# Gathering a unit's rows earlier on the GpSimd queue of a fused decoder block

## The chip, the core and the metric

The kernel runs on one core of a Trainium2 chip. The metric is device time in microseconds (us). Before the change it is 1564.48 us, the median of 3 runs (1563.86 to 1565.02). The profile is one execution, taken by the hardware profiler. Its engines are PE (TensorE: matrix products and transposes; PEld is its weight load), DVE (VectorE), ACT (ScalarE), POOL (GpSimd) and SP (SyncE, which here only issues DMAs). Each engine works through its own list of instructions in order; semaphores join the lists.

## The reference

One decoder layer over 512 tokens of width 1024: a mixer (sparse attention beside a pooling branch), then a mixture of experts, each followed by a LayerNorm. The change touches the experts alone:

```python
logits = (hf @ w_router).astype(jnp.float32) + b_router.astype(jnp.float32)
top_logit, top_e = lax.top_k(logits, TOP_K_EXPERTS)          # 4 of 32
gate = jax.nn.softmax(top_logit, axis=-1)
...
gu = xb @ w_gate_up[e] + b_gate_up[e]                         # xb: the expert's tokens
x_glu, x_lin = jnp.split(gu, 2, axis=-1)
x_glu = jnp.minimum(x_glu, SWIGLU_LIMIT)
x_lin = jnp.clip(x_lin, -SWIGLU_LIMIT, SWIGLU_LIMIT)
act = x_glu * jax.nn.sigmoid(SWIGLU_ALPHA * x_glu) * (x_lin + 1.0)
return act @ w_down[e] + b_down[e]
```

Each token's four results are weighted by `gate` and summed. Everything is float32; one expert's weights are 12 MB.

## The kernel before

The mixer fills the first 450 us or so; the rest are 32 *jobs*, one for each expert, ranked by how many tokens chose it. `KINDS` (line 63) gives every job a shape. A narrow job (N) has at most 64 tokens: its products use the weights as they were loaded, line 1404. A wide job (W) has at most 128: each weight chunk is first split into a high and a low part, by ACT (line 225) and DVE (line 234), and PE makes three products, line 1394. A triple job (T, jobs 8 and 19) is two *units* in one, a wide and a narrow one. All other jobs are one unit. The kinds in order are NNNNNNNN T NN WWWWW NNN T NN WWWW N WWW NN.

**Phases.** A job j has an up phase ("G", j), eight weight chunks of 1 MB, and a down phase ("D", j), four. `phases_of` interleaves them: ..., G j, D j-1, G j+1, D j, ...; around a triple job two of one kind follow each other (D 7, G 8, G 9, D 8, G 10, D 9, G 11, D 10, ...). A phase begins on PE with a product for the bias, line 1421. The weights are loaded by SP into a ring of tiles (`raw`), always a certain number of chunks ahead: a chunk's load is issued when an older chunk has been used up.

**A unit's rows.** A unit's tokens are found by a list of row numbers (`sl_wr`) and gate weights (`sl_gt`), which DVE writes for four units at a time (`unit_batch`, lines 1261 to 1278). `gather` (line 1373) is an indirect DMA that POOL issues: it fetches the listed rows from DRAM (`h2_rows`, shown as h_rows) into the tile `xg`. There is room for one unit there, or two of a triple job, so a gather waits on POOL until PE has transposed the rows that lay there before. `turn_steps` are those transposes (line 1331, from xg to a PSUM bank `ps_c`), four for a narrow unit and eight for a wide one, and the copies to `xT` or `xTn` (lines 1345, 1347, 1348). They are hooked into the down phase that stands before the unit's own up phase: job j's rows are turned in D j-2.

**What POOL does besides.** In the up phase's wake two swiglu products (lines 1464, 1465) of each half, and for each down phase `finish_down`: ACT copies the result out of PSUM, scaled (line 1489), POOL multiplies it by gate2 (line 1491 for a wide result in tile `y`, line 1495 in two halves for a narrow one in `yn` or `y`), and an indirect DMA adds it to the rows of `acc_rows` in DRAM (line 1470, the scatter).

**What sets the order.** `hook(ph, k, f)` runs f behind chunk k of phase ph, and the order in which the hooks run is the order of instructions on every engine. The swiglu of an up phase and `finish_down` of a down phase come behind all hooks of their phase. Before the change a unit's gather is hooked to chunk 0 of the phase before the one in which its rows are turned (`late_hook`), behind all other hooks of that chunk.

Of the kernel before, what the change touches and what calls it, by code (L numbers as in the profile page):

```python
# [36 lines left out]
E = 32  # L37
# [33 lines left out]
def tile_hybrid_block(ctx, tc, x, c, w_ada, b_ada, w_in, kv_norm_g, w_uk, w_uv, w_pool_group,  # L71
# [24 lines left out]
    def slot(shape, tag, dt=F32, bufs=1, name=None):  # L96
        pool = stream if tag in LASTING else ft_last if tag in LAST else ft
        return pool.tile(shape, dt, name=name or tag, tag=tag, bufs=bufs)
# [68 lines left out]
    def phases_of():  # L167


        order, late = [], None  # L170
        for j in range(E):
            if j in TRIPLE + (FIRST, E - 1):
                order += [late, ("G", j)]
            else:
                order += [("G", j)] + ([late] if late else [])
            late = ("D", j)
        return order + [late]
# [334 lines left out]
    units = [("ki", split_ki, whole, HD + H, True)]  # L512
# [225 lines left out]
    up, us = slot([P, PAD + S], "u"), slot([P, 2, PAD + S], "usum")  # L738
# [54 lines left out]
    for g in range(4):  # L793
# [12 lines left out]
        for i in range(2):  # L806
            n = 2 * g + i
            v = yb[n // 4][:, n % 4, :]
# [227 lines left out]
    phases = phases_of()  # L1036
# [210 lines left out]
    def mt(shape, tag, dt=F32, bufs=1, name=None):  # L1247
        return (mp if tag in AT_ONCE else mp_rest).tile(shape, dt, name=name or tag, tag=tag, bufs=bufs)
# [32 lines left out]
    def units_of(j):  # L1281
        return [(j, b) for b in range(1 + (j in TRIPLE))]

    def is_narrow(unit):
        return unit[0] in NARROW or unit[1] > 0

    units = [u for j in range(E) for u in units_of(j)]
# [25 lines left out]
    def unit_batch(us):  # L1313
        def col(i):
            j, b = units[us[i]]
            place = pos1[:, :, BASE + j] if j < FIRST else moe["place"][:, :, j]
            if b == 0:
                return place
            second = mt([P, NT], "second")
            nc.vector.tensor_scalar(second, place, float(P), None, op0=OP.subtract)  # L1320
            return second
        return batch(us, col, lambda i, t: aux[:, t, units[us[i]][0], :], 
                     narrow=[is_narrow(units[u]) for u in us])
# [37 lines left out]
    def shared_tile():  # L1361

        if not shared:
            shared.append(stream.tile([P, 2048], F32, name="xg", tag=ROWS[0], bufs=1))
            nc.gpsimd.memset(shared[0][:, 0:1536], 0.0)
        return shared[0]

    def gather(key, narrow, second=False):

        at = 1024 if second else 0  # L1370
        assert all(at != v[0] for v in held.values())
        v = shared_tile()[:, at:at + (512 if narrow else 1024)]
        nc.gpsimd.indirect_dma_start(out=v, out_offset=None, in_=in_halves if narrow else h2_rows[:, :],
                                     in_offset=bass.IndirectOffsetOnAxis(ap=lists[key][0], axis=0),
                                     bounds_check=(2 * S if narrow else S) - 1, oob_is_err=False)
        held[key] = at, v
# [274 lines left out]
    v = mt([P, 1, 3], "sl_v0")  # L1651
# [29 lines left out]
    def hook(ph, k, f):  # L1681
        hooks[ph].setdefault(k, []).append(f)

    gathers = []

    def late_hook(*args):
        gathers.append(args)

    first_unit = {j: units.index((j, 0)) for j in range(E)}
    xTs, acts, aTs = {(0, 0): xT}, {}, {}  # L1690

    def turn_steps(unit):

        fs, narrow = [], is_narrow(unit)

        def begin():
            xTs[unit], steps = gathered(units.index(unit), narrow, unit[1] > 0 or unit[0] in (1, FIRST + 1))
            fs.extend(steps)
            fs.pop(0)()
        return [begin] + [lambda: fs.pop(0)() for _ in range(1 if narrow else 3)]  # L1700

    def act_steps(unit):

        fs, narrow = [], is_narrow(unit)

        def begin():
            aTs[unit] = act_pair(unit[1] > 0 or unit[0] + 1 in TRIPLE + (FIRST, E - 1), narrow)
            for i in range(1 if narrow else 2):
                fs.extend(half_T(acts[unit][i], aTs[unit], i))
            fs.pop(0)()  # L1710
        return [begin] + [lambda: fs.pop(0)() for _ in range(1 if narrow else 3)]

    def spread(ph, ks, steps):
        for i, f in enumerate(steps):
            hook(ph, ks[i * len(ks) // len(steps)], f)

    for i, (kind, j) in enumerate(phases):
        before = phases[i - 1]
        if kind == "G" and j:
            at, ks = before, (0, 1, 1, 2) if before[0] == "D" else (4, 5, 5, 6)  # L1720
            if j in TRIPLE:
                at, ks = ("G", j - 1), (3, 4, 4, 5, 6, 7)
            elif j - 1 in TRIPLE:
                at, ks = ("D", j - 2), (0, 1)
            spread(at, ks, [f for u in units_of(j) for f in turn_steps(u)])
            if j > 1:
                for u in units_of(j):
                    late_hook(phases[phases.index(at) - 1], 0, lambda u=u: gather(units.index(u), is_narrow(u), u[1] > 0))
        elif kind == "D" and j < E - 1:
            spread(before, (3, 4, 5, 6, 6, 7) if j in TRIPLE else (1, 2, 2, 3) if before[0] == "G" else (3,), [f for u in units_of(j) for f in act_steps(u)])  # L1730
    first, second = unit_batch([1]), unit_batch([2])
# [3 lines left out]
    u = 3  # L1735
    while u < len(units):
        j = units[u][0]
        us = list(range(u, min(u + NB, len(units))))
        fs = unit_batch(us)
        for k, f in zip((0, 1, 2, 3), fs[:-2]):  # L1740
            hook(("G", j - 2), k, f)
        hook(("G", j - 2), 4, fs[-2])
        hook(phases[phases.index(("G", j - 2)) + 1], 0, fs[-1])
        u = us[-1] + 1
    for args in gathers:
        hook(*args)
    for j in range(1, E):
        if KINDS[j] != "W":
            hook(("G", j - 1), 2, lambda j=j: pick_halves(j))
# [24 lines left out]
    for ph in phases:  # L1774
        kind, j = ph
        last, us = j == E - 1, units_of(j)
# [132 lines left out]
```

## Time and profile before

| | |
|---|---|
| median of 3 runs | 1564.48 us |
| the profiled execution | 1565.03 us, span 1563.2 us |
| PE busy | 1451.2 us, 93% of the span |
| DVE, ACT, POOL busy | 58%, 40%, 30% |
| granted TensorE clock, mean | 0.970 of full speed |
| DMA | 489.96 MB, mean 313 GB/s |
| gathers of line 1373 | 33 |

The profile shows spans of instructions, and before each the idle time of its engine and what ended it. Issuing a DMA counts as busy on POOL; the transfer itself runs on the core's 16 DMA engines, and its landing is what others wait for. The DMA share in the windows view is the mean busy share of these engines; it can pass 1 a little.

### The profile page before, as it was taken

The numbers are of one execution on the slowest core, as the hardware profiler recorded it, in microseconds if no ns is written. First come the engines' busy times: TensorE is split into PE (matmuls) and PEld (weight loads), VectorE is DVE, ScalarE is ACT, GpSimd is POOL, SyncE is SP. The second block draws the span as 40 slices with busy tenths as digits, with TensorE's granted clock in tenths as the row PEclk, the third lists the DMA queues.
The fourth block names the chain that finished last, engine by engine and source line by source line (L and its number), as shares of the span: only waits on it lengthen the run. The fifth ranks groups of instructions, "written<-read, shape, count | busy, mean of one in ns | idle before, by whom it ended". The sixth has DMA issues, their size and how long they took to land. (4 is left out here: it accounts for less than half of the span.)

```text
span 1563.2 us, 18968 instructions
## 1 busy us (share of the span) xinstructions
PE 1451.2 (93%) x6821; PEld 884.6 (57%) x6821; DVE 913.4 (58%) x1262; ACT 626.5 (40%) x725; POOL 467.0 (30%) x338
## 2 busy tenths in 40 slices
PE   7999999998979998789889999999988999999995
PEld 6766766667843332244356777434435677567551
DVE  6558877567843111054159999404415899589613
ACT  2344234462111101143147776314314677567521
POOL 2200000023522232223324444332232444444332
PEclk8999999999969999999999999999998999999998
DMA  9874521044679999999999899999989989999993
GB/s 290 265 253 135 190 91 55 29 135 189 229 253 416 406 403 410 409 408 362 328 400 404 328 369 363 365 398 406 400 321 386 404 310 365 363 403 395 370 393 137
DMA packets 123377, 489.96 MB, mean 313 GB/s; under 512 B 12513, under 2 KB 42861, under 8 KB 88464
## 3 DMA queue, kind: packets, MB, share of 16 engines
q1 hardware_dynamic: 110832, 445.25, 72.8%
q0 software_dynamic: 12304, 43.27, 9.5%
q8 instruction: 55, 0.90, 0.2%
q14 instruction: 42, 0.34, 0.1%
q10 hardware_dynamic: 144, 0.20, 0.0%
HBM read 473.36 MB, written 19.20 MB: 315 GB/s over the span
## 5 line engine op out<-in xcount | busy, mean ns | idle before, releaser
L234 DVE TENSOR_TENSOR w_lo<-raw,w_hi 128x2048 fp32r<-128x2048 f32 x168 | 419.4, 2520 | 93.9 <-ACT w_hi L225 93.8
L225 ACT ACTIVATE w_hi<-raw 128x2048 fp32r<-128x2048 f32 x168 | 320.2, 1914 | 110.2 <-PE ps_a L1394 91.5
L1404 PE MATMUL ps_a<-raw,xTn 128*64 128x512 f32 x1024 | 237.4, 606 | 11.4 <-DMA raw<-in_w_gate_up_dram 11.4
L1394 PE MATMUL ps_a<-w_hi,xT 128*128 128x512 f32 x896 | 234.0, 404 | 3.5 <-ACT w_hi L225 3.5
L1464 POOL TENSOR_TENSOR sw_l<-sw_l,sw_g 128x512 f32<-128x512 f32 x47 | 88.3, 1879 | 447.6 <-DVE sw_l L1461 393.9
L1394 PEld LDWEIGHTS ps_a<-w_hi,xT 128*128 128x128 f32 x896 | 166.4, 190 | 54.0 <-ACT w_hi L225 11.4
L563 PE MATMUL ps_a<-h_part,wp 128*128 128x512 f32 (+1 forms) x672 | 167.3, 404 | 3.6 <-POOL h_part L500 2.1
L1459 DVE TENSOR_SCALAR sw_g<-ps_a 128x512 f32<-128x512 f32 x46 | 31.6, 687 | 235.1 <-PE ps_a L1404 199.6
L1404 PEld LDWEIGHTS ps_a<-raw,xTn 128*64 128x64 f32 x1024 | 68.8, 138 | 145.2 <-issue 119.8
L563 PEld LDWEIGHTS ps_a<-h_part,wp 128*128 128x128 f32 (+1 forms) x672 | 125.5, 189 | 45.0 <-issue 11.3
L1404 PE MATMUL ps_b<-raw,aT 128*64 128x512 f32 x576 | 137.3, 610 | 11.8 <-DMA raw<-in_w_down_dram 10.0
L1394 PE MATMUL ps_a<-w_lo,xT 128*128 128x512 f32 x448 | 124.3, 400 | 1.8 <-DVE w_lo L234 1.8
L1394 PE MATMUL ps_b<-w_hi,aT 128*128 128x512 f32 x448 | 125.8, 403 | 0.0
L1394 PEld LDWEIGHTS ps_a<-w_lo,xT 128*128 128x128 f32 x448 | 84.8, 190 | 24.3 <-DVE w_lo L234 4.3
L1460 ACT ACTIVATE sw_l<-ps_a,ones 128x512 f32<-128x512 f32 x46 | 31.4, 682 | 161.9 <-PE ps_a L1404 109.9
L1394 PEld LDWEIGHTS ps_b<-w_hi,aT 128*128 128x128 f32 x448 | 81.5, 188 | 23.0 <-issue 6.2
L1404 PEld LDWEIGHTS ps_b<-raw,aT 128*64 128x64 f32 x576 | 37.6, 138 | 87.1 <-issue 59.8
L1495 POOL TENSOR_TENSOR yn<-yn,gate 64x512 f32<-64x512 f32 x30 | 49.5, 1650 | 111.2 <-ACT yn L1489 87.8
L1465 POOL TENSOR_TENSOR sw_l<-sw_l,xg 128x512 f32<-128x512 f32 x47 | 75.1, 1597 | 3.7
L1394 PE MATMUL ps_b<-w_lo,aT 128*128 128x512 f32 x224 | 70.8, 398 | 1.5 <-DVE w_lo L234 1.5
L1348 DVE TENSOR_TENSOR xT<-ps_c,xT 128x512 fp32r<-128x512 f32 x28 | 19.1, 683 | 72.1 <-ACT xT L1347 72.1
L1491 POOL TENSOR_TENSOR y<-y,gate 128x1024 f32<-128x1024 f32 x14 | 37.7, 2693 | 75.7 <-ACT y L1489 75.7
(400 smaller groups left out, 1914.2 us busy)
## 6 DMA issues: line engine op xcount, KB each, us to landing
raw<-in_w_gate_up_dram SPq DMA_DIRECT2D x256, 1024.0 KB, 11.7
raw<-in_w_down_dram SPq DMA_DIRECT2D x128, 1024.0 KB, 9.2
ada<-in_w_ada_dram POOLq DMA_DIRECT2D x16, 1024.0 KB, 5.3
raw<-in_w_in_dram SPq DMA_DIRECT2D x14, 1024.0 KB, 9.0
raw<-in_w_ada_dram SPq DMA_DIRECT2D x32, 256.0 KB, 5.4
raw<-in_w_out_dram SPq DMA_DIRECT2D x4, 1024.0 KB, 5.4
x<-in_x_dram SPq DMA_DIRECT2D x8, 256.0 KB, 7.8
raw<-in_w_branch_pool_dram SPq DMA_DIRECT2D x2, 1024.0 KB, 5.3
```

The lines of the kernel that those rows point to most:

```text
L225: nc.scalar.activation(c["hi"], c["w"], AF.Copy)
L234: nc.vector.tensor_sub(c["lo"], c["w"], c["hi"].bitcast(F32))
L563: nc.tensor.matmul(ps, w[:, part, k, :], h(k), start=(k == part == 0 and h is hh), stop=(k == last and h is hl))
L1348: nc.vector.tensor_sub(pair[:, 1, ks, :], ps[0], pair[:, 0, ks, :].bitcast(F32))
L1394: nc.tensor.matmul(ps[i], a[:, part, k + j, :], m[:, cs], start=first and j == 0 and part == 1, stop=last and j == 4 // n - 1 and m is lo)
L1404: nc.tensor.matmul(ps[i][h * 64:(h + 1) * 64], a[:, kk, c * 64:(c + 1) * 64], w["w"][:, cs], start=first and j == 0, stop=last and j == 4 ...
L1459: nc.vector.tensor_scalar(g, ps[i], LIMIT, None, op0=OP.min)
L1460: nc.scalar.activation(l, ps[len(ps) // 2 + i], AF.Identity, bias=ones[:, 0:1])
L1464: eng.tensor_mul(l, l, g)
L1465: eng.tensor_mul(l, l, sig)
L1491: nc.gpsimd.tensor_mul(y, y, gate2)
L1495: nc.gpsimd.tensor_mul(y[rows], y[rows], gate2[rows, h * 512:(h + 1) * 512])
```

## The change

A unit's gather is now hooked to the place at which the rows of the preceding job have been turned (`turned[j - 1]`: the phase and the last chunk of those steps), or to the place at which its own list is made (`listed`), whichever is later. The hooks are still added last.

```diff
-    gathers = []
-
-    def late_hook(*args):
-        gathers.append(args)
-
     first_unit = {j: units.index((j, 0)) for j in range(E)}
+    listed = {2: (phases.index(("G", 1)), 2)}
...
+    turned = {}
     for i, (kind, j) in enumerate(phases):
...
             spread(at, ks, [f for u in units_of(j) for f in turn_steps(u)])
-            if j > 1:
-                for u in units_of(j):
-                    late_hook(phases[phases.index(at) - 1], 0, lambda u=u: gather(units.index(u), is_narrow(u), u[1] > 0))
+            turned[j] = phases.index(at), ks[-1]
...
-        hook(phases[phases.index(("G", j - 2)) + 1], 0, fs[-1])
+        after = phases.index(("G", j - 2)) + 1
+        hook(phases[after], 0, fs[-1])
+        listed.update({v: (after, 0) for v in us})
         u = us[-1] + 1
-    for args in gathers:
-        hook(*args)
+
+    for j in range(2, E):
+        for u in units_of(j):
+            p, k = max(turned[j - 1], listed.get(units.index(u), (0, 0)))
+            hook(phases[p], k, lambda u=u: gather(units.index(u), is_narrow(u), u[1] > 0))
```

On PE, DVE, ACT and SP the same instructions stand in the same order as before. On POOL they differ in where the gathers (line 1373) stand. The first place is POOL around jobs 8 to 11, from the swiglu of triple job 8 on; the two gathers are those of job 10 (128x512) and of job 11, the first wide one (128x1024). Before:

```order
L1465 TENSOR_TENSOR sw_l<-sw_l,xg 128x512
L1373 DMA xg<-h_rows,sl_wr 128x512
L1464 TENSOR_TENSOR sw_l<-sw_l,sw_g 128x512
L1465 TENSOR_TENSOR sw_l<-sw_l,xg 128x512
L1491 TENSOR_TENSOR y<-y,gate_3549 128x1024
L1470 DMA acc_rows<-y,sl_wr 640x1024
L1495 TENSOR_TENSOR yn<-yn,gate_3549 64x512 x2
L1470 DMA acc_rows<-yn,sl_wr 1280x512
L1373 DMA xg<-h_rows,sl_wr 128x1024
L1464 TENSOR_TENSOR sw_l<-sw_l,sw_g 128x512
```

The same place of POOL's list after the change:

```order
L1465 TENSOR_TENSOR sw_l<-sw_l,xg 128x512
L1373 DMA xg<-h_rows,sl_wr 128x512
L1464 TENSOR_TENSOR sw_l<-sw_l,sw_g 128x512
L1465 TENSOR_TENSOR sw_l<-sw_l,xg 128x512
L1373 DMA xg<-h_rows,sl_wr 128x1024
L1491 TENSOR_TENSOR y<-y,gate_3549 128x1024
L1470 DMA acc_rows<-y,sl_wr 640x1024
L1495 TENSOR_TENSOR yn<-yn,gate_3549 64x512 x2
L1470 DMA acc_rows<-yn,sl_wr 1280x512
L1464 TENSOR_TENSOR sw_l<-sw_l,sw_g 128x512
```

The gather of job 11 has moved ahead of both results of job 8 and their scatters; job 10's has not moved. The same ten rows stand around jobs 19 to 22.

The second place is POOL in the early run of narrow jobs, the gathers of jobs 6 and 7 and of the two units of triple job 8. Before:

```order
L1495 TENSOR_TENSOR yn<-yn,gate_3549 64x512 x2
L1470 DMA acc_rows<-yn,sl_wr 1280x512
L1373 DMA xg<-h_rows,sl_wr 128x512
L1464 TENSOR_TENSOR sw_l<-sw_l,sw_g 128x512
L1465 TENSOR_TENSOR sw_l<-sw_l,xg 128x512
L1495 TENSOR_TENSOR yn<-yn,gate_3549 64x512 x2
L1470 DMA acc_rows<-yn,sl_wr 1280x512
L1373 DMA xg<-h_rows,sl_wr 128x512
L1464 TENSOR_TENSOR sw_l<-sw_l,sw_g 128x512
L1465 TENSOR_TENSOR sw_l<-sw_l,xg 128x512
L1373 DMA xg<-h_rows,sl_wr 128x1024
L1373 DMA xg<-h_rows,sl_wr 128x512
```

And after:

```order
L1373 DMA xg<-h_rows,sl_wr 128x512
L1495 TENSOR_TENSOR yn<-yn,gate_3549 64x512 x2
L1470 DMA acc_rows<-yn,sl_wr 1280x512
L1464 TENSOR_TENSOR sw_l<-sw_l,sw_g 128x512
L1465 TENSOR_TENSOR sw_l<-sw_l,xg 128x512
L1373 DMA xg<-h_rows,sl_wr 128x512
L1495 TENSOR_TENSOR yn<-yn,gate_3549 64x512 x2
L1470 DMA acc_rows<-yn,sl_wr 1280x512
L1464 TENSOR_TENSOR sw_l<-sw_l,sw_g 128x512
L1465 TENSOR_TENSOR sw_l<-sw_l,xg 128x512
L1373 DMA xg<-h_rows,sl_wr 128x1024
L1373 DMA xg<-h_rows,sl_wr 128x512
```

Here a gather has changed places with the multiply and the scatter in front of it; those of the triple job stay.

## Rows read from the trace of the kernel before

**Rows 1.** Waits of PE, whole run: engine, line, for whom: us in total, times, longest.
```profile
PE ps_c L1331 <- DMA xg<-h_rows,sl_wr: 20.3, 3, 10.0
```
**Rows 2.** PE's timeline, jobs 8 to 11: start us, us, instruction [idle before, ended by].
```profile
743.33 0.66 PE L1331 MATMUL ps_c<-ident,xg 128*128 128x128 f32 x4
...
773.58 0.50 PE L1421 MATMUL ps_b<-bias,pick_n 128*128 128x512 f32 x1
...
785.62 1.08 PE L1331 MATMUL ps_c<-ident,xg 128*128 128x128 f32 x4 [9.67 <-DMA xg<-h_rows,sl_wr]
...
793.66 0.73 PE L1421 MATMUL ps_a<-bias,p_pick 64*128 64x512 f32 x4
```
**Rows 3.** PE's timeline, jobs 20 to 22.
```profile
1164.75 0.50 PE L1421 MATMUL ps_b<-bias,pick_n 128*128 128x512 f32 x1
...
1177.12 1.09 PE L1331 MATMUL ps_c<-ident,xg 128*128 128x128 f32 x4 [10.00 <-DMA xg<-h_rows,sl_wr]
...
1185.67 0.73 PE L1421 MATMUL ps_a<-bias,p_pick 64*128 64x512 f32 x4
```
**Rows 4.** PE's timeline, job 10's down phase and the start of the next.
```profile
817.19 0.40 PE L1421 MATMUL ps_b<-bias,pick_n 128*128 128x512 f32 x1
...
826.01 0.73 PE L1421 MATMUL ps_a<-bias,p_pick 64*128 64x512 f32 x4
```
**Rows 5.** POOL's timeline, jobs 8 to 11.
```profile
728.58 1.07 POOL L1373 DMA_INDIRECT xg<-h_rows,sl_wr  x1 [0.15 <-DVE sl_gt L1277]
...
742.91 1.27 POOL L1465 TENSOR_TENSOR sw_l<-sw_l,xg 128x512 f32<-128x512 f32 x1
...
760.30 1.60 POOL L1470 DMA_INDIRECT acc_rows<-y,sl_wr  x1 [0.28 <-POOL y L1491]
...
770.43 1.27 POOL L1495 TENSOR_TENSOR yn<-yn,gate 64x512 f32<-64x512 f32 x1 [7.23 <-DMA acc_rows<-y,sl_wr]
...
773.88 1.09 POOL L1373 DMA_INDIRECT xg<-h_rows,sl_wr  x1 [0.30 <-PE ps_a L1404]
```
**Rows 6.** POOL's timeline, jobs 20 to 22.
```profile
1134.09 1.26 POOL L1465 TENSOR_TENSOR sw_l<-sw_l,xg 128x512 f32<-128x512 f32 x1
...
1165.96 1.06 POOL L1373 DMA_INDIRECT xg<-h_rows,sl_wr  x1 [0.30 <-issue]
```
**Rows 7.** Line 1373: duration ns min/median/max; who waited for it, us, times; landing.
```profile
L1373 POOL DMA_INDIRECT xg<-h_rows,sl_wr x33: 1010/1077/2956, 455.3 to 1491.2; - x33
...
  POOL yn L1495: 7.2, 3
  POOL y L1495: 6.3, 1
...
DMA to landing us min/median/max: 2.9/10.0/13.1
```
**Rows 8.** Windows: stretch, us, busy us of engines, PEclk (granted clock), DMA share, GB/s.
```profile
776.00:786.00 10.00, 0.38 (x2) 0.41 (x3) 0.00 (x0) 0.00 (x0) 1.56 (x2) 0.62 1.03 394
786.00:986.00 200.00, 196.64 (x891) 143.04 (x891) 175.14 (x134) 134.21 (x109) 85.50 (x40) 0.99 0.96 367
986.00:1066.00 80.00, 76.98 (x363) 30.97 (x359) 18.37 (x27) 18.55 (x23) 26.02 (x18) 1.00 1.02 397
...
1178.00:1478.00 300.00, 296.59 (x1343) 209.97 (x1344) 248.45 (x183) 194.18 (x158) 125.11 (x59) 0.99 0.97 375
```
**Rows 9.** SP's issues of job 11's up weights, and the page's landing of such loads.
```profile
762.66 13.67 SPq L139 DMA_DIRECT2D raw<-in_w_gate_up_dram  x8
...
raw<-in_w_gate_up_dram SPq DMA_DIRECT2D x256, 1024.0 KB, 11.7
```
**Rows 10.** POOL's timeline in the early narrow run.
```profile
564.19 1.27 POOL L1465 TENSOR_TENSOR sw_l<-sw_l,xg 128x512 f32<-128x512 f32 x1
...
573.57 1.59 POOL L1470 DMA_INDIRECT acc_rows<-yn,sl_wr  x1 [0.28 <-POOL yn L1495]
...
599.76 2.60 POOL L1495 TENSOR_TENSOR yn<-yn,gate 64x512 f32<-64x512 f32 x2 [7.27 <-ACT yn L1489]
```

## The prediction

> **What bounds the kernel now.** I read the list of what TensorE (PE) waited for first. Its longest entry is a pair of waits of some 10 us each, by the row transposes of line 1331 for the landing of a gather (xg<-h_rows): 20.3 us over three times [rows 1]. Then the PE timeline around them. The first stands in job 9's down phase, 775.95 to 785.62, before the transposes of job 11's rows; the second in job 20's, 1167.12 to 1177.12, before job 22's [rows 2, 3]. Both are the first wide job after the two triple jobs (8 and 19). What has to be seen there is that the transposes stand after the first of the phase's four weight chunks, so the three others wait behind them on PE although they need nothing of the gather.
>
> The POOL timeline says why the gather is late [rows 5]. It stands behind job 8's two results (the multiplies by gate2 and the scatters); the second half of the second multiply waited 7.23 us until the first scatter had landed (770.43), and the gather left at 773.88. Its list was made long before: the gather of job 10, whose list belongs to the same batch of four, left at 728.58 as soon as that batch's last row was written. Job 10's rows were turned at 743.33 to 743.99 [rows 2].
>
> Last the windows of the weight stream [rows 8]. From 786 to 986, the first run of wide jobs, the DMA engines are busy 0.96 of the time and from 1178 to 1478 0.97, while a run of narrow jobs (986 to 1066) shows 1.02, the full stream. So PE sets the pace after either wait, and the stream has some time to spare, though little.
>
> **The change, part by part.** PE, VectorE, ScalarE and the SP queue hold the same instructions in the same order in both kernels. On POOL no instruction is added or taken out; 25 of the main loop's 33 gathers move forward: 18 past one multiply and its scatter, 4 past a swiglu pair, the last past a multiply, its scatter and a swiglu pair, and those of jobs 11 and 22 past two multiplies and two scatters.
>
> *Jobs 11 and 22.* In its new place the gather of job 11 waits for three things: its list (done by 728.58), the landing of the gather before (728.58 plus 13.1 at the longest, 741.7) and the transposes of job 10's rows (743.99). POOL itself is free at 742.91 + 1.27 = 744.18 [rows 5]. So it leaves near 744.2 instead of 773.88, and lands at 757.3 with the longest landing seen [rows 7], 18.6 us before PE asks at 775.95. For job 22 POOL is free at 1134.09 + 1.26 = 1135.35 [rows 6]; 13.1 later is 1148.5, also 18.6 us before 1167.12. Neither wait remains in part.
>
> What they cost now is read from the whole phase, since PE came back slow. Job 9's down phase lasts from bias to bias 793.66 - 773.58 = 20.08 us and job 20's 1185.67 - 1164.75 = 20.92 [rows 2, 3]. Job 10's, with the same narrow products and the same turning of wide rows but no wait, lasts 826.01 - 817.19 = 8.82 [rows 4]. The differences are 11.26 and 12.10, together 23.4 us. The bare waits are 9.67 + 10.00 = 19.7; the other 3.7 is the clock. PE did no matmul from 776 to 785, the granted clock of that stretch is 0.62, between the levels 2.4 and 1.2 GHz [rows 8], and after it four transposes took 1.08 us, where the four at 743.33 took 0.66 [rows 2]. That part cannot be less than nothing; it is 3.7 if PE is never idle there and keeps its clock, which I take.
>
> *Is what follows ready 11 us earlier?* Job 11's eight weight chunks are issued from 762.66 on; with the median landing of 11.7 the first is there at 774.4 [rows 9], when the split into hi and lo could start at about 777. They are just in time, with a later chunk perhaps waiting a microsecond, so between 0 and some 5 us of the gain may be lost at once. I take 0.4, and 23.0 for both places.
>
> *Does the stream follow?* PE's lead eats into loaded chunks, and the stream must win it back before the next narrow run, where PE is held by weights. Spare from 786 to 986 is (1.02 - 0.96) x 200 = 12 us, for 11.3 needed; from 1178 to 1478 it is (1.02 - 0.97) x 300 = 15, for 12.1 [rows 8]. Both suffice, the first barely. The bounds are nothing lost and everything lost (23 us); I take nothing, since the idle shares stand in the wide runs, in which buffers are released by PE's progress and would be released earlier too.
>
> *The other 23 moved gathers.* No PE wait stands before their transposes except 0.6 us (20.3 - 9.67 - 10.00). So there is nothing to win: I take 0, and 0.6 is the most. The four that move ahead of a swiglu hold it for one issue, 1.08 us [rows 7], if anything; in their place POOL is idle before the products arrive. 0.
>
> *The added wait.* POOL's multiply of a narrow result, in its second half, waits for the gather in front of it: that is where the 7.2 and 6.3 us in [rows 7] come from. Now that gather is a younger one. In the narrow run around 570, POOL is free at 564.19 + 1.27 = 565.5; a gather issued then lands at 575.5 (median) or 578.6 (longest), so the half that ended at 573.3 would end by 579.9 at the latest and the scatter of 573.57 would leave 6.6 us later. Behind it stand the next swiglu (a job later) and ScalarE's next write into the yn tile, which ended at 599.76 [rows 10]. A scatter took 10.1 us until its release (760.30 to 770.43), so yn is free by 590.3: 9 us of cover. Cost 0. Without that cover it would be paid by PE, see the last rival.
>
> A rule of the Trainium skill speaks against moving gathers into the wide runs. The row first: VectorE is busy 175 of the 200 us after 786 [rows 8], and a gather's issue took POOL 1.08 us in the median and 2.96 at the longest [rows 7]. "SBUF — State Buffer", section "SBUF: two separate sides", says that POOL cannot write the descriptors of such a DMA while VectorE holds the shared port pair. By the rows that is under 2 us more per gather, ahead of a wide multiply; by the rule it could be a whole VectorE instruction or several, and it is why I give the slower side 4 chances and not 2.
>
> The sum: the profiled execution took 1565.03 us (span 1563.2 and 1.8 around it), 0.55 above the median of the runs shown. 1565.0 - 23.0 = 1542.0.
>
> **The rivals.**
> *The stream takes part of it back.* PE runs ahead and then waits for weights, in the wide run or in the narrow jobs behind it. For: the first spare (12) hardly exceeds the need, the shares are rounded to 0.01 (2 us in 200), and job 11's chunks come just in time. Against: buffers full in either run. If half of the spare is usable, 6 + 7.5 = 13.5 us is won: 1551.5.
> *No gain.* The gather leaves no earlier in fact, because something else that it waits for at its new place is late, or because PE is held for as long by another wait after the transposes. For: a wait for several semaphores is put down to one only. Against: all three known releases lie before 744. Time: 1565, within 3 us.
> *Slower.* The younger gather holds POOL's narrow multiply, scatters slip past the next use of yn, ScalarE's copy out of PSUM waits and PE's next down phase with it. It decides from a landing of 13.1 + 9 = 22 us. The price with 26 us (twice the longest) would be 4 us in each of the ten narrow results behind a moved gather: +40 - 23 = +17, 1582. For: gathers and the weight stream share the engines, and the wait exists already. Against: 13.1 is the longest of 33 landings, many of them in a full stream.
>
> **How the numbers follow.** The forecast 0.78 (its own range 1539 to 1547: a microsecond or two more from small waits, 5 less if job 11's chunks come late), the stream 0.13, no gain 0.05, slower 0.04. 0.2% is about 3 us, what the measurement can tell from no change. Faster 0.91, same 0.05, slower 0.04. For 8 in 10 the range reaches from 1538 into the stream's case, to 1555; past that lie the last two rivals and a part of the first.
>
> **What would show it.** Right: no entry of line 1331 waiting 10 us for xg; job 9's and job 20's down phases 8.8 to 9.5 us long; the granted clock not falling there; the DMA share from there to the next narrow run near 1.0 instead of 0.96; POOL's waits of its narrow multiplies for xg grown from 13.5 us (7.2 + 6.3) to a few tens with no PE wait behind them. Wrong: longer PE waits for raw after 960 (the stream), or a wait of the same length in the same phases with another name (no gain), or ScalarE's copies of yn waiting for scatters in several phases (slower).

## The result, and the profile after

The changed kernel takes 1542.13 us, the median of 4 runs (1540.63 to 1542.84), against 1564.17 (4 runs) before: ratio 0.9864, 95% interval 0.9849 to 0.9879, a gain of 22.0 us. The forecast was 1542.0. Its parts did not all come out so exactly, as the experiments show.

PE's timeline of the changed kernel at the places of [rows 2, 3] (start us, us, instruction): job 9's down phase and its end, then job 20's.

```profile
769.60 0.50 PE L1421 MATMUL ps_b<-bias,pick_n 128*128 128x512 f32 x1
...
771.90 0.66 PE L1331 MATMUL ps_c<-ident,xg 128*128 128x128 f32 x4
...
778.52 0.72 PE L1421 MATMUL ps_a<-bias,p_pick 64*128 64x512 f32 x4
...
1150.66 0.50 PE L1421 MATMUL ps_b<-bias,pick_n 128*128 128x512 f32 x1
...
1152.96 0.66 PE L1331 MATMUL ps_c<-ident,xg 128*128 128x128 f32 x4
...
1159.58 0.73 PE L1421 MATMUL ps_a<-bias,p_pick 64*128 64x512 f32 x4
```

Both phases now last 8.92 us from bias to bias, where they lasted 20.08 and 20.92. No wait stands before either group of transposes, and four of them take 0.66 us instead of 1.08. The head of the list of PE's waits, whose first entry was [rows 1]:

```profile
PE ps_a L1404 <- DMA raw<-in_w_gate_up_dram: 12.0, 16, 1.4
PE ps_b L1404 <- DMA raw<-in_w_down_dram: 8.3, 14, 1.4
PE ps_a L1394 <- DVE w_lo L234: 4.6, 6, 1.1
```

The entry for xg is gone. The waits for weights (raw) have not taken its place; they were 11.4 and 10.0 us. The third line was 1.8 us over 5 times before: this is new, and the experiments come back to it.

POOL's timeline where [rows 5] stood:

```profile
738.93 1.27 POOL L1465 TENSOR_TENSOR sw_l<-sw_l,xg 128x512 f32<-128x512 f32 x1
740.35 2.92 POOL L1373 DMA_INDIRECT xg<-h_rows,sl_wr  x1
753.68 2.36 POOL L1491 TENSOR_TENSOR y<-y,gate 128x1024 f32<-128x1024 f32 x1 [10.42 <-ACT y L1489]
...
766.46 1.27 POOL L1495 TENSOR_TENSOR yn<-yn,gate 64x512 f32<-64x512 f32 x1 [7.21 <-DMA acc_rows<-y,sl_wr]
...
775.28 2.96 POOL L1373 DMA_INDIRECT xg<-h_rows,sl_wr  x1 [1.72 <-PE ps_c L1331]
779.55 1.71 POOL L1495 TENSOR_TENSOR yn<-yn,gate 64x512 f32<-64x512 f32 x1 [1.31 <-ACT yn L1489]
785.96 1.29 POOL L1495 TENSOR_TENSOR yn<-yn,gate 64x512 f32<-64x512 f32 x1 [4.70 <-DMA xg<-h_rows,sl_wr]
```

Job 11's gather leaves at 740.35, as soon as POOL is free, 31 us before PE asks for its rows. Its issue takes 2.92 us, not 1.09. The last line is the added wait: the second half of a narrow multiply waits 4.70 us for the gather that now stands in front of it (issued at 775.28). Line 1373 over the whole run, as in [rows 7]:

```profile
L1373 POOL DMA_INDIRECT xg<-h_rows,sl_wr x33: 1017/1073/2958, 455.0 to 1444.0; - x33
...
  POOL yn L1495: 26.3, 9
  POOL y L1495: 4.9, 1
...
DMA to landing us min/median/max: 2.9/7.8/10.5
```

POOL's waits for gathers have grown from 13.5 to 31.2 us (26.3 + 4.9), and no wait of PE or ScalarE has come of it. The windows that answer to [rows 8] (the columns are the same); the two wide runs are taken from some us into G 11 and G 22 on:

```profile
769.00:779.00 10.00, 10.00 (x49) 3.36 (x45) 5.72 (x6) 6.22 (x7) 6.10 (x4) 1.00 1.03 395
787.00:962.00 175.00, 170.03 (x768) 129.17 (x767) 159.72 (x112) 120.00 (x95) 77.86 (x35) 0.99 0.99 385
962.00:1042.00 80.00, 79.06 (x373) 33.84 (x373) 24.49 (x43) 19.34 (x24) 31.74 (x19) 1.00 1.00 385
1174.00:1444.00 270.00, 264.99 (x1205) 192.50 (x1205) 232.03 (x172) 175.20 (x142) 114.72 (x53) 0.99 1.00 390
```

The granted clock stays at 1.00 in the first. In the wide runs the DMA share is 0.99 and 1.00; before it is 0.96 and 0.97, in [rows 8] as in the same work cut alike (802 to 976 and 1200 to 1469): the spare of the stream has been used up, and it was enough.

### The profile page after: what moved, and what is told of

Its sections match the earlier page's. It is cut to its first block, busy times and chain, and to the rows that moved or that the text cites. A ratio compares the mean times of both kernels' runs of the same rounds, so it can differ in the third digit from the quotient of the medians.

```text
span 1538.9 us, 18966 instructions
## 1 busy us (share of the span) xinstructions
PE 1448.2 (94%) x6821; PEld 885.0 (58%) x6821; DVE 916.1 (60%) x1262; ACT 626.4 (41%) x725; POOL 480.9 (31%) x338
## 5 line engine op out<-in xcount | busy, mean ns | idle before, releaser
L1404 PE MATMUL ps_b<-raw,aT 128*64 128x512 f32 x576 | 134.8, 601 | 10.5 <-DMA raw<-in_w_down_dram 8.3
L1495 POOL TENSOR_TENSOR yn<-yn,gate 64x512 f32<-64x512 f32 x30 | 46.4, 1548 | 93.2 <-ACT yn L1489 51.2
L1373 POOL DMA_INDIRECT xg<-h_rows,sl_wr x33 | 55.1, 1668 | 25.8 <-PE ps_c L1331 9.7
L506 DVE TENSOR_TENSOR wp<-raw,wp 128x1024 fp32r<-128x1024 f32 x29 | 37.7, 1310 | 26.3 <-ACT wp L505 26.2
```

The lines of the kernel that those rows point to most:

```text
L506: eng.tensor_sub(pair[:, 1], view, pair[:, 0].bitcast(F32))
L1404: nc.tensor.matmul(ps[i][h * 64:(h + 1) * 64], a[:, kk, c * 64:(c + 1) * 64], w["w"][:, cs], start=first and j == 0, stop=last and j == 4 ...
L1495: nc.gpsimd.tensor_mul(y[rows], y[rows], gate2[rows, h * 512:(h + 1) * 512])
```

## The experiments

Each kernel from the third row on ran 4 to 12 times, beside the kernel before on the same chip; ratios are to those runs. Phase lengths are from bias to bias on PE's timeline, in one profiled execution each.

| kernel | median us | ratio, 95% interval | D 9, D 20 | G 14, 15, 25, 29 |
|---|---|---|---|---|
| before | 1564.17 | | 20.1, 20.9 | 24.6, 24.5, 24.6, 24.5 |
| changed | 1542.13 | 0.9864 (0.9849 to 0.9879) | 8.9, 8.9 | 25.4, 25.3, 25.4, 25.3 |
| changed, again | 1542.23 | 0.9858 (0.9839 to 0.9876) | 8.9, 8.9 | 25.3, 25.4, 25.4, 25.4 |
| changed, third | 1543.33 | 0.9862 (0.9842 to 0.9882) | 8.9, 8.9 | 25.4, 25.3, 25.3, 25.3 |
| jobs 11, 22 only | 1538.87 | 0.9838 (0.9824 to 0.9852) | 8.9, 8.9 | 24.6, 24.5, 24.6, 24.5 |
| the same, again | 1538.92 | 0.9837 (0.9819 to 0.9854) | 8.9, 8.9 | 24.5, 24.6, 24.5, 24.5 |
| the other 23 only | 1565.21 | 1.0008 (0.9997 to 1.0019) | 21.6, 20.9 | 25.3, 25.3, 25.3, 25.3 |
| behind the multiply | 1539.27 | 0.9841 (0.9826 to 0.9855) | 8.9, 8.9 | 24.5, 24.5, 24.6, 24.5 |
| the same, again | 1539.06 | 0.9841 (0.9823 to 0.9859) | 8.9, 8.9 | 24.6, 24.5, 24.5, 24.5 |
| early and two | 1540.19 | 0.9842 (0.9823 to 0.9861) | 8.9, 8.9 | 24.6, 24.6, 24.5, 24.5 |

**The two gathers alone.**

```diff
             p, k = max(turned[j - 1], listed.get(units.index(u), (0, 0)))
+            if j not in (11, 22):
+                p, k = turned[j][0] - 1, 0
```

> The change for jobs 11 and 22 alone; the other 23 moved gathers stand where they stood before. Theory A (the gain is job 9's and job 20's down phases, 11.2 + 12.0 us shorter; the other moved gathers cost 4.7 us, because five up phases of wide runs, G 12, 14, 15, 25 and 29, are 0.8 to 1.5 us longer, where a gather now stands in front of POOL's wide multiply): faster than the changed kernel by about 4 to 5 us, 1537 to 1538; both down phases 8.9 us, the five up phases as before the change (26.6, 24.6, 24.5, 24.6, 24.5). Theory B (these five up phases are longer because PE runs 11 us further ahead of the weight stream and of the splitting, whatever POOL does): as the changed kernel, 1542, the five up phases as long as there (28.1, 25.4, 25.3, 25.4, 25.3). Theory C (the other gathers were worth something too, hidden in the profile): slower than the changed kernel, 1545 or more.

It measured 1538.87, 25.9 us under the 1564.82 of its own comparison, and 3.3 under the changed kernel, where theory A had 4 to 5. The four up phases G 14, 15, 25 and 29 are back at 24.5 and 24.6: theory A for these, and B and C are out. G 12 stayed at 28.1 and was wrongly on the list: in the next run of this same kernel it was 26.6, so it comes and goes by itself.

**The other 23 alone** (the same lines with `j in (11, 22)`).

> The other 23 moved gathers alone; those of jobs 11 and 22 stand where they stood before. Theory A (the other gathers cost 4.7 us in five up phases of wide runs and win nothing): slower than the kernel before by 4 to 5 us, 1568 to 1569, with both PE waits of 10 us still there. Theory B (the longer up phases come of PE's lead, which is missing here): 1564, up phases as before the change. Theory C (they win by themselves): under 1561.

The four up phases are long here too, although PE has no lead, which is against B once more. PE's waits are headed by

```profile
PE ps_c L1331 <- DMA xg<-h_rows,sl_wr: 20.3, 2, 10.4
```

so both waits remain. But the whole costs 0.4 us (interval -0.5 to +3.0), not theory A's 4 to 5. The four phases show 4 x 0.8 = 3.2; something else gives most of it back here, and no run shows what.

**What makes the four phases long.** In the changed kernel a wide job's gather stands in front of POOL's multiply of the wide result. In this kernel it stands behind that multiply and ahead of the scatter (`between` holds the gathers of the phase):

```diff
                 nc.gpsimd.tensor_mul(y, y, gate2)
+                for f in between:
+                    f()
```

> The whole change, but in down phases of wide jobs the gather stands behind POOL's multiply of the wide result (line 1491) and ahead of its scatter, not ahead of both. If the up phases of the wide runs grew because the gather's issue of up to 2.9 us pushes that multiply into VectorE's split (line 234): up phases 14, 15, 25 and 29 back at 24.5 to 24.6 us, some 3 us faster than the changed kernel, 1539. If it is the gather's issue itself that holds VectorE, wherever it stands: the phases stay at 25.3 to 25.4 and the time at 1542.

1539.27, and the phases are back. The timelines of POOL, VectorE and PE at the start of G 14 show how (start us, us). Before:

```profile
903.77 0.73 PE L1421 MATMUL ps_a<-bias,p_pick 64*128 64x512 f32 x4
...
904.99 2.42 POOL L1491 TENSOR_TENSOR y<-y,gate 128x1024 f32<-128x1024 f32 x1 [2.34 <-ACT y L1489]
905.33 4.23 DVE L234 TENSOR_TENSOR w_lo<-raw,w_hi 128x2048 fp32r<-128x2048 f32 x1
...
909.61 1.20 PE L1394 MATMUL ps_a<-w_lo,xT 128*128 128x512 f32 x4 [0.26 <-DVE w_lo L234]
```

The changed kernel:

```profile
889.21 2.94 POOL L1373 DMA_INDIRECT xg<-h_rows,sl_wr  x1 [0.15 <-issue]
...
890.17 0.73 PE L1421 MATMUL ps_a<-bias,p_pick 64*128 64x512 f32 x4
...
891.73 5.02 DVE L234 TENSOR_TENSOR w_lo<-raw,w_hi 128x2048 fp32r<-128x2048 f32 x1
892.18 2.41 POOL L1491 TENSOR_TENSOR y<-y,gate 128x1024 f32<-128x1024 f32 x1
...
896.80 1.20 PE L1394 MATMUL ps_a<-w_lo,xT 128*128 128x512 f32 x4 [1.05 <-DVE w_lo L234]
```

The gather behind the multiply:

```profile
893.69 2.42 POOL L1491 TENSOR_TENSOR y<-y,gate 128x1024 f32<-128x1024 f32 x1 [2.34 <-ACT y L1489]
894.03 4.23 DVE L234 TENSOR_TENSOR w_lo<-raw,w_hi 128x2048 fp32r<-128x2048 f32 x1
...
896.26 2.93 POOL L1373 DMA_INDIRECT xg<-h_rows,sl_wr  x1 [0.16 <-PE ps_a L1394]
...
898.31 1.19 PE L1394 MATMUL ps_a<-w_lo,xT 128*128 128x512 f32 x4 [0.29 <-DVE w_lo L234]
```

An undisturbed split takes 2.29 us (the median of the 168 of line 234). Each of these three ends 2.15 to 2.16 us after POOL's multiply ends (907.41, 894.59, 896.11): in each, VectorE's split does its work only when the multiply is done. In the changed kernel the gather's issue of 2.94 us stands ahead, so the multiply ends 4.42 us after the phase's bias product instead of 3.64, the split 0.8 later, PE's wait for w_lo grows from 0.26 to 1.05, and the phase by 0.8. Behind the multiply the issue is just as long (2.93), the multiply ends 3.64 us after the bias product (which starts at 892.47) as before the change, and PE's wait is 0.29. In the changed kernel a gather stands right in front of a wide multiply at thirteen places. At the start of these four up phases the issue takes 2.94 to 2.96 us and ends when the result y is already there; at the other nine the multiply still waits 0.97 to 10.42 us for y (ScalarE, line 1489), so the issue delays nothing. "SBUF — State Buffer", section "SBUF: two separate sides", in the Trainium skill calls the port pair of VectorE and POOL an exclusive lock, held for a whole instruction; that split and multiply follow each other whole agrees with it. Why the split comes second in the changed kernel too, where its span begins 0.45 us before the multiply's and beside the issue, is not shown.

**How much of the stall is the clock.** The kernel before, with products of the identity in front of the transposes of jobs 11 and 22, `FILL` of them, 84 at first:

```diff
+    for j in (9, 20):
+        hook(("D", j), 0, lambda: keep_warm(FILL))
```

> The kernel before, with 84 products of the identity (128x128, into a bank that nobody reads) on PE in front of the row transposes of jobs 11 and 22, where PE waited 9.7 and 10.0 us for the gather; at 0.11 us each at full clock they fill 9.2 us of either wait. The wait itself stays. If the part of the two down phases beyond the bare waits (1.6 and 2.1 us) is the clock: job 9's and job 20's down phases 18.5 and 18.8 us instead of 20.1 and 20.9, granted clock 1.00 there, the time 3.5 us less, 1560.5. If that part is something else (weights, PSUM banks, the turning of wide rows): phases and time as before, 1564, or longer.

1576.01 (ratio 1.0074, interval 1.0059 to 1.0089), with both phases at 27.7: the filling was mis-sized. Each call is two PE instructions, and PE's timeline has

```profile
774.48 19.02 PE L581 MATMUL ps_c<-ident 128*128 128x128 f32 x168
793.34 0.60 PE L1331 MATMUL ps_c<-ident,xg 128*128 128x128 f32 x4
```

Again with 40 calls:

> The kernel before with 40 calls of the identity product in front of the row transposes of jobs 11 and 22, in place of 84: the run with 84 showed two PE instructions for each call, 168 in 19.0 us, so these 80 fill 9.06 us and fit into waits of 9.7 and 10.0 us. Clock theory (the part of the two phases beyond the bare waits is a clock that falls in the wait): down phases 9 and 20 take 18.3 and 18.7 us instead of 20.1 and 20.9, the time is 4 us less than the kernel before, about 1560.5. Otherwise: phases and time as before, 1564.5.

1560.56, ratio 0.9977 (0.9965 to 0.9989): 4.1 us won (interval 1.7 to 5.5) by keeping PE busy with products that nobody reads.

```profile
769.18 0.50 PE L1421 MATMUL ps_b<-bias,pick_n 128*128 128x512 f32 x1
...
771.47 9.20 PE L581 MATMUL ps_c<-ident 128*128 128x128 f32 x80
781.98 0.63 PE L1331 MATMUL ps_c<-ident,xg 128*128 128x128 f32 x4 [1.31 <-DMA xg<-h_rows,sl_wr]
...
788.58 0.74 PE L1421 MATMUL ps_a<-bias,p_pick 64*128 64x512 f32 x4
```

The phases were expected at 18.3 and 18.7 and are 19.4 and 19.5, since the gather came later against PE here: 9.20 of filling and a wait of 1.31. What is left, 19.40 - 1.31 - 9.2 = 8.9, is the length of the phase without a stall (the second: 19.46 - 1.37 - 9.2 = 8.9), and the granted clock from 771 to 781 is 1.00. In the kernel before, 20.08 - 9.67 = 10.4 was left. So 1.5 us of that stall was the clock, and of the second 20.92 - 10.00 - 8.92 = 2.0. The two phases together are 2.1 us shorter than before; the rest of the 4.1 is not seen in them, and lies within the interval.

**A landing twice as long.** To try the slower rival, the 13 gathers hooked to a narrow job's down phase are issued twice into one tile, so that the second waits for the first to land:

```diff
-            hook(phases[p], k, lambda u=u: gather(units.index(u), is_narrow(u), u[1] > 0))
+            for _ in range(2 if phases[p][0] == "D" and KINDS[phases[p][1]] == "N" else 1):
+                hook(phases[p], k, lambda u=u: gather(units.index(u), is_narrow(u), u[1] > 0))
```

> The changed kernel, but the 13 gathers that stand in front of a narrow multiply or behind another such gather are issued twice into the same tile; the second waits on POOL for the first to land, so the multiply behind it waits for two landings, some 8 us more. It adds 6 x 0.25 + 7 x 0.5 = 5.0 MB of traffic, 2.5 MB of it in stretches with a full weight stream, 6 us at 397 GB/s. Forecast (the younger gather is covered by some 9 us until the next use of the yn tile): 1542 plus at most the 6 us of traffic and a few us, 1542 to 1551. Rival 'slower' of the prediction (a landing of over 22 us holds the multiply, the scatter and the next copy into yn, 4 us a place): 1580 or more, with ScalarE's copies of line 1489 waiting for scatters and PE behind them.

1544.94, ratio 0.9877 (0.9860 to 0.9893): 2.7 us over the 1542.23 of the changed kernel beside it. POOL's waits were

```profile
POOL xg L1373 <- DMA xg<-h_rows,sl_wr: 97.2, 13, 8.5
...
POOL yn L1495 <- DMA xg<-h_rows,sl_wr: 48.7, 10, 5.6
...
POOL y L1495 <- DMA xg<-h_rows,sl_wr: 4.9, 1, 4.9
```

together 151 us instead of 31. ScalarE's only wait for a scatter is 11.4 us, once, as before the change (11.1). PE waits for xg three times, 10.2 us in all, for rows that land twice. So the cover of some 9 us behind the narrow multiplies is there, and 8 us more of landing do not exhaust it. PE's waits themselves show that the price of a stall depends on its place: two of them, 5.0 us each, made G 2 and G 18 7.3 and 6.8 us longer, but from G 2 up to G 8 PE took 4.3 us more than in the changed kernel and from G 17 up to G 19 3.4, since later phases of the same narrow runs, where PE waits for weights, came out shorter (G 5 15.9 instead of 19.7).

**How far the two gathers have to move.** In the kernel before, they are put between the triple job's two results (`between` is the gather of job 11 or 22):

```diff
             add_rows(y, wr, len(ps) == 1)
+            if between and len(ps) == 2:
+                between()
```

> The kernel before, but the gathers of jobs 11 and 22 stand between the two results of the triple jobs 8 and 19: behind the wide multiply and its scatter, ahead of the narrow multiply. They leave about 762 instead of 774 (12 us earlier; 744 in the changed kernel) and land 10 to 13 us later, 772 to 775, just before PE asks at 776. If 10 us are all that is needed: 1539 as with the full move of these two, no wait left over 1 us. If the landing is later behind the scatter's traffic or the narrow multiply, which now waits for this gather, holds up what follows: a PE wait of 1 to 4 us stays in one or both phases, 1541 to 1546.

1540.80, ratio 0.9841 (0.9821 to 0.9860), with no wait over 1 us for rows: as far as these runs can tell, 12 us earlier do as well as 30. The narrow multiply pays:

```profile
761.04 1.07 POOL L1373 DMA_INDIRECT xg<-h_rows,sl_wr  x1 [0.30 <-issue]
...
773.22 1.28 POOL L1495 TENSOR_TENSOR yn<-yn,gate 64x512 f32<-64x512 f32 x1 [9.80 <-DMA xg<-h_rows,sl_wr]
```

ScalarE's copies into yn then waited 9.3 us for scatters, in two places, and G 11 took 24.5 instead of 23.5: here the cover ends. PE's wait in G 11 (0.82 us) is for a split of VectorE, which had waited for ScalarE's work behind the late copy.

**The early moves, and all on one chip.** The last four kernels shared a chip and the runs of the kernel before (1564.36). The first moves jobs 2 to 8, 11 and 22:

```diff
+            if 8 < j < 11 or 11 < j < 22 or j > 22:
+                p, k = turned[j][0] - 1, 0
```

> The moves of the early narrow run (jobs 2 to 8) and of jobs 11 and 22; all others as before. The profiles with the whole change show phases D 1 and D 7 0.6 to 0.7 us shorter, G 5 and G 7 some 0.4 to 0.8 longer and G 8 42.6 where 43.9 to 46.3 stand in most profiles without the moves. If that is the moves' doing: 1 to 2 us under the kernel with jobs 11 and 22 alone, 1537. If it comes and goes from run to run: the same as that kernel, 1539.

> Jobs 11 and 22 alone, beside the changed kernel on one chip. If the four up phases at 0.8 us are a real cost of the whole change: 1539, 3 us less than the changed kernel. If it was the chip: no difference, both near 1540.5.

> The changed kernel on the same chip as the three others: 1542 if the 3 us between it and the kernel with jobs 11 and 22 alone are real, else as that kernel.

> The whole change with the gathers of the wide runs behind the wide multiply, on the same chip as the three others: 1539, as the kernel with jobs 11 and 22 alone, and 3 us less than the changed kernel, if only the multiply's place in the wide runs costs.

The second measured 1538.92 (1536.75 to 1539.99), the third 1543.33 (1541.59 to 1543.68), the fourth 1539.06 (1537.66 to 1541.66). In the second and third the runs do not overlap, so the difference is not the chip's. An earlier repeat of the changed kernel, beside other kernels, had said the same of itself (1542.23):

> The changed kernel once more, beside the others on one chip: 1542, which is 3 us over the run in which only jobs 11 and 22 move (1538.9) and over the one with the gathers behind the wide multiply (1539.3), if the four up phases of 25.3 us cost what they showed. If the 3 us were the difference of chips or of runs: 1539.

The first gave 1540.19 (1537.35 to 1542.24): the early moves win nothing that can be measured.

## Why the prediction was right, and where its steps were off

**The gather leaves earlier and the wait goes.** Right: POOL is free at the place named and the gather gone at once, 29.3 us before job 9's down phase begins (forecast 773.58 - 744.2 = 29.4), and with the longest landing, now 10.5, the rows are there 21 us early (forecast 18.6). *No gain* is out.

**The price of the two phases, 23.4 us.** 20.08 - 8.92 and 20.92 - 8.92 make 23.2 in the two profiles, and the part laid to the clock was 3.7, measured 3.5 (1.5 + 2.0) by the filled waits. The runs give more: jobs 11 and 22 alone win 25.9 and 25.4, interval 23 to 28 us. In the kernel with the other 23 moves job 9's phase lasted 21.6 with a wait of 9.9, so the stall varies and may be longer than in the one profile; that this is all of it was not shown.

**Job 11's chunks in time, 0.4 lost.** Nothing was lost: G 11 lasts 23.5 in both kernels.

**The stream follows.** Right, and the rival *the stream takes part of it back* is out: its share rose to 0.99 and 1.00, the waits for weights did not grow.

**The other 23 gathers, 0.** This is the step that failed. They cost 3.3 to 4.4 us in the whole change (1542.2 and 1543.3 against 1538.9), 3.2 of it seen in four up phases. The prediction had the right size for the issue, under 2 us more beside VectorE's splits (2.94 instead of 1.07, less than one split of 2.29 more), and left it without consequence. What it did not follow is the instruction behind the issue: a multiply of 2.4 us that VectorE's next split has to wait out, in phases where PE already waits for that split (0.26 us). It was named as a reason for the slower side; it is no slowdown but a loss inside the gain. That the 23 alone lost only 0.4 us is open. In their profile G 8 takes 42.7 at a clock of 1.00 in its first stretch, where before it took 46.3 at 0.77; but with only the early moves G 8 is as short (42.8) and the time no better. Over all profiles G 8 lasts 42.4 to 42.8 in the eight with the early moves and 42.8 to 46.3 in the six without, so some gain there may offset the loss; that was not shown.

**The sum.** That 1542.0 was met to 0.1 us is luck: by the medians two errors cancelled. The two gathers win 2 to 3 us more than the forecast 23.0 (which lies at the edge of their interval), the others lose 3 to 4. The own profile of before also held 3.7 us in G 8 that the profile after did not; a difference of two profiles, 24.3 us, is not the 22.0 of the runs.

**Slower.** Not only absent but far: with landings twice as long ScalarE waited for scatters no more than before, and the whole cost 2.7 us in place of 4 us a place; PE's two waits of 5.0 us are for the rows themselves. That ScalarE's copies wait once the cover is exhausted was seen between the two results, where the multiply was held 9.8 us. How much cover there is depends on the place: held 7.7 us there (by the first scatter, in one profile of jobs 11 and 22 alone), the copy came just as the scatter landed. The 9 us were worked out for the early narrow run, and no run exhausted them there.

**What is faster than both.** Moving the two gathers alone, 1538.9, or putting the wide runs' gathers behind the multiply, 1539.1 to 1539.3: 3 to 4 us under the changed kernel.

## What to carry to other kernels

Price a stall by its whole phase against the same phase without one, since the engine can come back at a lower clock (3.5 of 23.2 us here), and look whether a later wait gives part of it back, as in the narrow runs. When an instruction moves forward in a queue, follow the one it pushes back: an issue that is harmless by itself can push a multiply into another engine's way. Move only what someone waits for; here two of 25 moves carried the gain, and the others took back a seventh of it.

## What the runs showed of the hardware

A POOL issue of an indirect DMA took 1.01 to 1.13 us with VectorE idle and up to 2.96 beside its splits. A split of VectorE takes 2.29 us in the median; beside a POOL multiply of 2.4 us its span was 4.23 to 5.02, and it ended 2.15 us after the multiply. PE with nothing to do for 10 us came back at 1.08 us for four transposes, the granted clock of that stretch being 0.62 [rows 8]; 80 products that nobody reads kept it at 0.63 and a clock of 1.00, and were worth 4.1 us of run time (1.7 to 5.5).
